# Neighbourhood attention with float16 pairs: probabilities turned by DMA instead of by TensorE

## The chip, the cores and the metric

The kernel runs on one core of one Trainium2 chip. The metric is the device time of one execution, in microseconds (us). The median of three runs before the change is 1503.19 us (1502.85 to 1503.6). The engines are PE (TensorE, matrix products; PEld is its weight load), DVE (VectorE), ACT (ScalarE), POOL (GpSimd) and SP (SyncE, which issues nearly all DMAs here, from one queue in order).

## The reference, cut to what matters

One layer of an encoder trunk on 1024 tokens of width 1024. Its token mixer has two halves, an mLSTM and a neighbourhood attention; their outputs are joined in one output projection. Then come a cross-attention and a gated FFN. Only the neighbourhood attention is changed. The tokens stand on a grid of 16 rows by 64 columns, there are 8 heads of width 64, and each token attends to a window of 8 rows by 16 columns:

```python
qg, kg, vg = grid(nq), grid(nk), grid(nv)
row_idx = jnp.clip(r - kr // 2, 0, rows - kr)[:, None] + jnp.arange(kr)[None, :]
k_rows = kg[:, :, row_idx].reshape(b, NA_HEADS, rows, kr * GRID_W, NA_DIM)
v_rows = vg[:, :, row_idx].reshape(b, NA_HEADS, rows, kr * GRID_W, NA_DIM)
s = jnp.einsum('bhrqd,bhrkd->bhrqk', qg, k_rows) * (NA_DIM ** -0.5)
...
s = jnp.where(mask, s + bias, -jnp.inf)
p = jax.nn.softmax(s, axis=-1)
o = jnp.einsum('bhrqk,bhrkd->bhrqd', p, v_rows)
```

All of it is float32 in the reference.

## The kernel before, in words

The kernel is written with a tile framework: the Python code names tiles and instructions, and a scheduler fixes, when the kernel is built, in which order each engine runs its instructions. At run time every engine goes through its own list in order and waits on semaphores. Products that need more than a 16-bit or a rounded 32-bit operand are made of two parts, high and low (`hi`, `lo`), and three matmuls (`mm3`: high by high, high by low, low by high). `split` makes such a pair with a copy on ACT and a subtraction on DVE; `split16` makes a pair of float16 with a scale `s`: ACT writes `hi = s*src`, DVE writes `lo = s*src - hi`.

The order of the program: layer norm and the token products (`tk`: values `nv`, output gates `mo`), the column products (`cu`, `cl`), the mLSTM, the neighbourhood attention, the second half of the output projection (`out`), the cross-attention, the FFN. Two parts of the program stand beside the change.

**The token products.** For `c` in 0 to 3 and 8 token tiles `tt`, PE makes a 128x256 product `tk`, DVE evicts it to `ev` (L819); for `c` below 2 `ev` is a part of the values and is stored as float32 to `nv` in DRAM.

**The neighbourhood attention** (`na_gen`, L1132 on). It runs over 4 head pairs `p` and 4 column blocks `cb`, 16 jobs in all. A job handles 16 columns of queries of two heads; these need 32 columns of keys. In a job:

- ACT and POOL split the queries (`qsh`, `qsl`) and the 16x32 keys (`kh`, `kl`, once per job) into pairs of float32r, and POOL subtracts bias from mask (`tb`, three jobs in four).
- The values `vt` are fetched with four DMAs (L1177).
- For each of 4 groups `g` of 4 query rows (8, 12, 12 and 8 key rows, so 256 or 384 keys): PE makes the scores `S` with `mm3`; DVE adds the table, takes the minimum of the negated scores and writes `P` (L1189); ACT takes the exponential and its sum (L1191); DVE inverts the sum (L1193) and scales `P` by it (L1194); PE turns `P` around in blocks of 128x128 (`tp`, L1199); ACT copies that to `PT` (L1201); PE multiplies with the values in float32 (`o`, L1203, two instructions each).
- ACT and DVE split the result into the pair `yna` (tiles `X2h`, `X2l`).

`mix` runs the first half of the output projection between these steps as filler for PE (`fill`, 16 products of 12 matmuls; L1072 loads a row tile, L1089 evicts on DVE, L1094 adds a bias on POOL, L1096 stores to `part`). Its second half, `out`, needs all of `yna`: product `k` of a row tile needs head pair `k`. It loads `part` back, and the cross-attention loads 4 MB of `kq` at the same time.

PSUM banks are named by letters: the scores have `Y` (3 banks), `o` has `X` (2), the filler has `Z` (1), and `tp` has 2.

## Time and profile before

| | |
|---|---|
| median of 3 runs | 1503.19 us (1502.85 to 1503.6) |
| profiled execution: its own time | 1502.08 us |
| profiled execution: span | 1500.0 us, so 2.08 us lie around the span |
| PE busy over the span | 1441.3 us (96%) |
| DVE, ACT, POOL busy | 1036.0 (69%), 825.7 (55%), 575.1 us (38%) |
| granted TensorE clock, mean | 0.992 |
| first and last L1189 (softmax) instruction start | 478.7 and 616.5 us |
| L1203 (products with values) | 487.2 to 629.3 us |

How to read it: PE is busy nearly all the time over the whole span, so a mean says little of the changed stage. The views to read are those cut to that stage, about 477 to 631 us, and to the token products, about 123 to 262 us. A row of the groups gives count, busy time and the mean of one instruction; a row of the windows gives the busy time of each engine in a stretch (PE, PEld, DVE, ACT, POOL, each with its count), the granted clock, the DMA share and GB/s; a row of the waits says who waited for whom, for how long in all, how often, and the longest. In the timeline, `xN` joins N like instructions in a row, and the second number is the time from the start of the first to the end of the last; matmuls overlap, so the distance of two starts is the time that one takes of PE.

### The profile page before, as it was taken

How to read it: one execution, taken by the hardware profiler on the slowest of the kernel's cores; microseconds unless marked ns; L12 is line 12 of the kernel's file. 1: busy time of each engine (PE TensorE's matmuls, PEld its weight loads, DVE VectorE, ACT ScalarE, POOL GpSimd, SP SyncE). 2: the span in 40 equal slices, each digit the busy share in tenths (PEclk: the TensorE clock that was granted, in tenths of full speed). 3: DMA queues.
4: the chain of work that ended last, by engine and by line, in shares of the span. 5: the costliest groups of instructions: out<-in, count | busy, mean ns of one | idle time of the engine just before them, and what ended most of it. 6: DMA issues, size and time to landing. Idle time of an engine off the chain costs nothing. (4 is left out here: it accounts for less than half of the span.)

```text
span 1500.0 us, 21659 instructions
## 1 busy us (share of the span) xinstructions
PE 1441.3 (96%) x8060; PEld 867.1 (58%) x8060; DVE 1036.0 (69%) x1945; ACT 825.7 (55%) x1393; POOL 575.1 (38%) x453
## 2 busy tenths in 40 slices
PE   8999999999999898999999799999999999999998
PEld 6998866456766887874444344444444444444444
DVE  7867866545777687488555868887787789707424
ACT  5766565655554666425444777787777767503000
POOL 5452357303325766045112454443444320300543
PEclk9999999999999999999999899999999999999999
DMA  8846653215544633644333233232233336713121
GB/s 308 318 163 215 197 186 129 84 49 151 164 124 156 206 127 127 239 155 71 85 71 100 88 138 126 113 126 113 113 118 119 143 114 239 271 36 99 48 76 59
DMA packets 116383, 208.61 MB, mean 139 GB/s; under 512 B 40627, under 2 KB 69555, under 8 KB 112950
## 3 DMA queue, kind: packets, MB, share of 16 engines
q1 hardware_dynamic: 115984, 206.47, 41.3%
q8 instruction: 63, 1.03, 0.3%
q0 software_dynamic: 144, 0.49, 0.2%
q14 instruction: 42, 0.34, 0.1%
q10 hardware_dynamic: 150, 0.27, 0.0%
HBM read 154.15 MB, written 45.15 MB: 133 GB/s over the span
## 5 line engine op out<-in xcount | busy, mean ns | idle before, releaser
L1527 POOL TENSOR_TENSOR wraw<-ur 128x512 f32<-128x512 f32 x22 | 45.9, 2085 | 207.1 <-issue 192.3
L225 PE MATMUL dn<-wlo,yp 128*128 128x512 f16 (+1 forms) x284 | 105.1, 370 | 0.0
L224 PE MATMUL dn<-whi,yp 128*128 128x512 f16 (+1 forms) x284 | 104.9, 370 | 0.0
L226 PE MATMUL dn<-whi,yp 128*128 128x512 f16 (+1 forms) x284 | 104.4, 370 | 0.0
L1615 DVE SCALAR_TENSOR_TENSOR cbuf<-C,wdw,cbuf 128x1024 f32<-128x1024 f32 x44 | 69.8, 1587 | 35.0 <-ACT cbuf L1614 34.8
L226 PEld LDWEIGHTS <-wlo 128*128 128x128 f16 x540 | 52.8, 98 | 56.5 <-DVE wlo L204 1.3
L225 PEld LDWEIGHTS <-whi 128*128 128x128 f16 x540 | 52.8, 98 | 55.9 <-issue 3.3
L224 PEld LDWEIGHTS <-whi 128*128 128x128 f16 x540 | 52.8, 98 | 53.1 <-ACT whi L203 0.3
L242 POOL TENSOR_TENSOR lnrs<-lnrs,mhalf 128x1 f32<-128x1 f32 x32 | 25.9, 809 | 137.9 <-DVE lnrs L241 132.2
L204 DVE SCALAR_TENSOR_TENSOR wlo<-wraw,us,whi 128x1024 f16<-128x1024 f32 (+1 forms) x48 | 62.5, 1320 | 18.7 <-ACT whi L203 18.7
L1616 DVE SCALAR_TENSOR_TENSOR cbuf<-C,wdw,cbuf 128x1024 f32<-128x1024 f32 x44 | 70.4, 1601 | 0.7
L252 ACT ACTIVATE r<-r,lnrs 128x1024 f32<-128x1024 f32 x19 | 23.6, 1239 | 78.3 <-DVE lnrs L251 78.0
L203 ACT ACTIVATE whi<-wraw,us 128x1024 f16<-128x1024 f32 (+1 forms) x48 | 51.2, 1102 | 16.4 <-DVE us L176 15.5
L225 PEld LDWEIGHTS <-yp 128*128 128x128 f16 x370 | 36.2, 98 | 39.9
L224 PEld LDWEIGHTS <-yp 128*128 128x128 f16 x370 | 36.2, 98 | 39.8
L1614 ACT ACTIVATE cbuf<-C,bdw,wdw 128x1024 f32<-128x1024 f32 x44 | 54.2, 1234 | 9.1 <-DVE C L1652 8.5
L226 PEld LDWEIGHTS <-yp 128*128 128x128 f16 x370 | 36.2, 98 | 39.7
L224 PE MATMUL tk<-whi,Bo 128*128 128x256 f16 (+1 forms) x192 | 52.6, 274 | 2.5 <-DVE stage L204 2.5
L224 PE MATMUL tk<-whi,Be 128*128 128x256 f16 (+1 forms) x192 | 52.6, 274 | 0.7 <-DVE stage L204 0.7
L225 PE MATMUL tk<-wlo,Be 128*128 128x256 f16 (+1 forms) x192 | 52.4, 274 | 0.8 <-DVE wlo L204 0.8
L225 PE MATMUL tk<-wlo,Bo 128*128 128x256 f16 (+1 forms) x192 | 52.5, 274 | 0.0
L226 PE MATMUL tk<-whi,Be 128*128 128x256 f16 (+1 forms) x192 | 52.5, 274 | 0.0
(526 smaller groups left out, 4892.1 us busy)
## 6 DMA issues: line engine op xcount, KB each, us to landing
ur<-in_w_up_dram SPq DMA_DIRECT2D x22, 1024.0 KB
sv<-in_w_down_dram SPq DMA_DIRECT2D x22, 512.0 KB
y<-cbuf SPq DMA_DIRECT2D x22, 512.0 KB
ur<-y SPq DMA_DIRECT2D x11, 1024.0 KB
wraw<-in_w_down_dram SPq DMA_DIRECT2D x22, 512.0 KB
r<-h SPq DMA_DIRECT2D x11, 512.0 KB
wraw<-in_w_tok_dram SPq DMA_DIRECT2D x10, 512.0 KB
wr<-in_w_xk_dram SPq DMA_DIRECT2D x8, 512.0 KB
```

The source lines that it names most:

```text
L203: A.activation(hi, src, AF.Copy, scale=s)
L204: return V.scalar_tensor_tensor(lo, src, s, hi, op0=OP.mult, op1=OP.subtract)
L224: T.matmul(ps, lh, rh, start=first, stop=False, skip_group_check=skip)
L225: T.matmul(ps, lh, rl, start=False, stop=False, skip_group_check=skip)
L226: return T.matmul(ps, ll, rh, start=False, stop=last, skip_group_check=skip)
L242: G.tensor_tensor(rs[:, 0:1], rs[:, 0:1], mhalf[:, 0:1], OP.pow)
L252: A.activation(r, r, AF.Identity, scale=rs[:, 0:1], bias=rs[:, 1:2])
L1527: G.tensor_tensor(S1, A21, A22, OP.add)
L1614: A.activation(c, C[:, 1:SEQ + 1], AF.Identity, scale=wdw[:, 1, j:j + 1], bias=bdw[:, j:j + 1])
L1615: V.scalar_tensor_tensor(c, C[:, 0:SEQ], wdw[:, 0, j:j + 1], c, op0=OP.mult, op1=OP.add)
L1616: V.scalar_tensor_tensor(c, C[:, 2:SEQ + 2], wdw[:, 2, j:j + 1], c, op0=OP.mult, op1=OP.add)
```

## The change

It makes these edits.

- Probabilities and values become float16 pairs. The scaling of `P` by the inverse sum (L1194) and the turning on PE (L1199) and the copy to `PT` (L1201) go. In their place `split16` writes `hl`, high and low, with the inverse sum times 2^14 as its scale, once for every two groups; and two DMA transposes per job, issued from SP, turn `hl` (128x1280 float16 each) to `PT`.
- The products with values go by key block: four blocks of 128 keys per job, each with all the groups that use it (256 or 384 columns), three float16 matmuls each. They run for job n-2 while job n is in work (`pv_gen`, yielded after the scores of job n).
- The values are brought to float16 pairs in the token stage: their largest magnitude is taken from `ev` (16 reductions on DVE), then each token tile is read back, split and written to a new scratch `nvp` (`nv_pair`, 8 times), laid out so that one DMA of 128 rows of 2 KB serves a job (`pv_load`, 16 in place of 64).
- The keys are split once per head pair (128x1024) and not once per job (128x512). The low part overwrites the raw tile.
- The filler has the two `tp` banks beside `Z`; it loads and stores its rows later (`late`); the second half of the output projection begins three row tiles with the products that need head pairs 0 to 2 (`lead`).

The diff, cut to its core:

```diff
-               fill="Z", fill2="ZX", ...
+               fill=["Z", "tp", "tp"], ...
+                    def nv_pair(tt):
+                        ...
+                        S.dma_start(f, nv_d[rows, :])
+                        hl = w1.tile([128, 4, 2, 128], F16, name="nvhl", tag="nvhl", bufs=2)
+                        split16(hl[:, :, 0], hl[:, :, 1], f.rearrange("p (k d) -> p k d", k=4), nvs[0][1])
+                        S.dma_start(... nvp_d ..., hl.rearrange("p k n d -> p k (n d)"))
                             if c < 2:
                                 S.dma_start(nv_d[tt * 128:(tt + 1) * 128, j], e)
+                                V.tensor_reduce(nvm[:, 8 * c + tt:8 * c + tt + 1], e, axis=mybir.AxisListType.X,
+                                                op=OP.max, apply_absolute_value=True)
+                            if c == 2 and tt == 1:
+                                nvs.append(scale_of(nvm, 14))
+                            if 8 * c + tt in range(18, 26):
+                                nv_pair(8 * c + tt - 18)
...
+            def pv_gen(n):
+                ...
+                for b in range(4):
+                    s0, g0, g1 = BG[b]
+                    vh, vl = vt[:, b, 0], vt[:, b, 1]
+                    ph, pl = (PT[:, i, s0:s0 + g1 - g0] for i in range(2))
+                    T.matmul(po[:, g0:g1], vh, ph, start=b == 0, stop=False, skip_group_check=True)
+                    T.matmul(po[:, g0:g1], vh, pl, start=False, stop=False, skip_group_check=True)
+                    anchor[0] = T.matmul(po[:, g0:g1], vl, ph, start=False, stop=b == 3, skip_group_check=True)
+                    yield 1
...
-                        kh = nw.tile([128, 16, 32], F32R, name="kh", tag="kh", bufs=2)
-                        kl = nw.tile([128, 16, 32], F32R, name="kl", tag="kl", bufs=2)
-                        A.activation(kh, kr[:, :, k0:k0 + 32], AF.Copy)
-                        (V if n < 2 else G).tensor_tensor(kl, kr[:, :, k0:k0 + 32], kh.bitcast(F32), OP.subtract)
+                        if cb == 0:
+                            kh = nw.tile([128, 16, 64], F32R, name="kh", tag="kh", bufs=2)
+                            kl = kr.bitcast(F32R)
+                            A.activation(kh, kr, AF.Copy)
+                            (V if n < 1 else G).tensor_tensor(kl, kr, kh.bitcast(F32), OP.subtract)
...
-                            V.reciprocal(mn[:, 1:2], mn[:, 1:2])
-                            V.tensor_scalar(P[:, :nk], P[:, :nk], mn[:, 1:2], None, op0=OP.mult)
+                            Ps.append((P, nk, m, g))
+                            if g % 2:
+                                V.reciprocal(mn[:, 1], mn[:, 1])
+                                V.tensor_scalar(mn[:, 1], mn[:, 1], 2.0 ** 14, None, op0=OP.mult)
+                                for P, nk, m, g_ in Ps:
+                                    nb = nk // 128
+                                    o = slice(GSLOT[g_], GSLOT[g_] + 2 * nb - 1, 2)
+                                    split16(hl[:, 0, o], hl[:, 1, o], P[:, :nk].rearrange("p (b t) -> p b t", b=nb),
+                                            m[:, 1])
-                            for b in range(nb):
-                                T.transpose(pt[:, b, :], P[:, b * 128:(b + 1) * 128], ident)
-                            A.activation(PT[:, :nb, :], pt[:, :nb, :], AF.Copy)
-                            for b in range(nb):
-                                anchor[0] = T.matmul(po[:, g, :], vt[:, r0 // 4 + b, :], PT[:, b, :], start=b == 0,
-                                                     stop=b == nb - 1)
+                        pts[n] = PT = nw.tile([128, 2, 10, 128], F16, name="PT", tag="PT", bufs=2)
+                        for i in range(2):
+                            S.dma_start_transpose(PT[:, i], hl[:, i].rearrange("p b t -> p (b t)"))
+                        if n > 1:
+                            yield from pv_gen(n - 2)
...
-            run(out_half(wB, ylk(yna), part0_d, None, None, "out", after1, todo=todo, home=home))
+            run(out_half(wB, ylk(yna), part0_d, None, None, "out", after1, todo=todo, home=home, lead=3))
```

The instruction lists of the two kernels differ most in three places. The first is DVE in the middle of the attention. Before, after each exponential DVE inverts one sum (L1193) and scales one `P` (L1194); the rows named ISA are the L1189 step and the reading of its minimum:

```order
L1189 ISA mn 128x1
L1193 RECIPROCAL mn<-mn 128x1
L1189 ISA P,mn<-S,tb_0_5428 128x256
L1189 ISA mn 128x1
L1194 TENSOR_SCALAR P<-P,mn 128x384
L1193 RECIPROCAL mn<-mn 128x1
L1194 TENSOR_SCALAR P<-P,mn 128x256
L1193 RECIPROCAL mn<-mn 128x1
L1194 TENSOR_SCALAR P<-P,mn 128x256
L1189 ISA P,mn<-S,tb_1_5429 128x384
```

Now the same place on DVE (L205 is the second instruction of `split16`, L1126 the eviction of the filler):

```order
L1277 RECIPROCAL mn<-mn 128x2
L1278 TENSOR_SCALAR mn<-mn 128x2
L205 SCALAR_TENSOR_TENSOR hl<-P,mn,hl 128x3x128
L205 SCALAR_TENSOR_TENSOR hl<-P,mn,hl 128x2x128
L1271 ISA P,mn<-S,tb_1_5511 128x384
L1271 ISA mn 128x1
L205 SCALAR_TENSOR_TENSOR X2l<-o,sc,X2h 64x16x16
L1271 ISA P,mn<-S,tb_3_5512 128x256
L1271 ISA mn 128x1
L1126 SCALAR_TENSOR_TENSOR r<-r,fill 128x512
L205 SCALAR_TENSOR_TENSOR hl<-P,mn,hl 128x2x128
L205 SCALAR_TENSOR_TENSOR hl<-P,mn,hl 128x3x128
```

One scaling of `P` per group has become one low part per group, which reads `P` and the high part and mostly stands next to that of the pair's other group, and one inversion with one small scaling now serve two groups.

The second place is SP's queue in the second half of the attention. Before:

```order
L1177 DMA vt<-nv 128x1x128 x4
L1096 DMA part_73<-r 128x1024
L1177 DMA vt<-nv 128x1x128 x3
L1072 DMA r<-h_72 128x1024
L1177 DMA vt<-nv 128x1x128 x7
L1096 DMA part_73<-r 128x1024
```

Now, at a like place:

```order
L1288 DMA_TRANSPOSE PT<-hl 128x10x128 x2
L1130 DMA part_73<-r 128x1024
L1213 DMA vt<-nvp 128x1x1024
L1094 DMA r<-h_72 128x1024
L1288 DMA_TRANSPOSE PT<-hl 128x10x128 x2
L1213 DMA vt<-nvp 128x1x1024
L1288 DMA_TRANSPOSE PT<-hl 128x10x128 x2
```

Four loads of values per job have become one, and two transposes per job, which wait for ACT's and DVE's parts of `hl`, stand between the loads and stores of the filler.

The third place is SP's queue at the end of the attention. Before, the 4 MB of `kq` stand behind the last loads of values:

```order
L1380 DMA whi<-vo 128x2048
L1380 DMA wlo<-vo 128x2048
L1177 DMA vt<-nv 128x1x128 x4
L1253 DMA kq_7242<-kq 128x4096 x2
L1253 DMA kq_7243<-kq 128x4096 x2
```

Now they stand behind the last four transposes:

```order
L1463 DMA wlo<-vo 128x2048
L1288 DMA_TRANSPOSE PT<-hl 128x10x128 x2
L1213 DMA vt<-nvp 128x1x1024
L1288 DMA_TRANSPOSE PT<-hl 128x10x128 x4
L1336 DMA kq_6991<-kq 128x4096 x2
L1336 DMA kq_6992<-kq 128x4096 x2
```

On PE, 27 matmuls of `out` and the products of jobs 13 and 14 now stand between the last scores and the products of job 15, and 36 of the 192 matmuls of `out` stand ahead of those; 18 more follow them that need only head pairs 0 to 2.

More of the change, by code (lines that the diff above doesn't have):

```diff
@@ L1058, in out_w, with out_half @@
                     for k in range(4)]
-        def out_half(w, y, res, dst, work, name, after=None, bias=None, rbufs=3, early=False, alpha=ALPHA, todo=range(NT), home=None):
+        def out_half(w, y, res, dst, work, name, after=None, bias=None, rbufs=3, early=False, alpha=ALPHA, todo=range(NT), home=None, late=False, lead=0):
             rs = {}
@@ L1074, in out_half, with part @@
             load_r(todo[0])
+            if late:
+                load_r(todo[1])
             yield 0
+            done, begun = [], {}
+            def part(ps, tt, ch, ks):
+                for k in ks:
+                    yh, yl = y(k, tt)
+                    wh, wl = w[k]
+                    cc = slice(ch * 512, ch * 512 + 512)
+                    mm3(ps, yh, yl, wh[:, 0, cc], wl[:, 0, cc], k == 0, k == 3)
+            for tt in todo[:lead]:
+                for ch in range(2):
+                    begun[tt, ch] = bank(name)
+                    part(begun[tt, ch], tt, ch, range(3))
             for n, tt in enumerate(todo):
-                if n + 1 < NT:
+                if n + 1 < NT and not late:
                     load_r(todo[n + 1])
@@ L1080, in out_half @@
                 for ch in range(2):
-                    ps = bank(name)
-                    for k in range(4):
-                        yh, yl = y(k, tt)
-                        wh, wl = w[k]
-                        cc = slice(ch * 512, ch * 512 + 512)
-                        mm3(ps, yh, yl, wh[:, 0, cc], wl[:, 0, cc], k == 0, k == 3)
+                    if (tt, ch) in begun:
+                        ps = begun[tt, ch]
+                        part(ps, tt, ch, (3,))
+                    else:
+                        ps = bank(name)
+                        part(ps, tt, ch, range(4))
                     rc = r[:, ch * 512:ch * 512 + 512]
@@ L1091, in out_half @@
                         V.tensor_tensor(rc, ps, rc, OP.add)
+                    if done and ch == 0:
+                        S.dma_start(*done.pop())
+                    if late and ch == 1 and 0 < n < NT - 1:
+                        load_r(todo[n + 1])
                     yield 1
@@ L1095, in out_half @@
                 if dst is not None:
-                    S.dma_start(dst[tt * 128:(tt + 1) * 128, :], r)
+                    done.append((dst[tt * 128:(tt + 1) * 128, :], r))
+                    if not late or n == NT - 1:
+                        S.dma_start(*done.pop())
                 if after is not None:
@@ L1220, in out_a @@
                 yield from out_half(wA, ylk(yml), h0_d, part0_d, nw,
-                                    "fill", bias=bmo, rbufs=2, early=True)
+                                    "fill", bias=bmo, rbufs=2, early=True, late=True)
                 with tc.issue_after(vload[0].ins):
```

83 lines of the change are left out of this document (55 added, 28 removed).

## The prediction, blind

> **What bounds the kernel now.** I cut the profile to the stages that the change touches and read the windows first. Columns: stretch, its length, then busy time and count of PE, PEld, DVE, ACT and POOL, granted clock, DMA share, GB/s.
>
> ```profile
> 123.00:195.00 72.00, 68.18 (x609) 59.31 (x608) 59.10 (x129) 40.61 (x67) 24.56 (x34) 1.00 0.61 192
> 195.00:262.00 67.00, 64.34 (x466) 45.55 (x465) 43.47 (x76) 36.51 (x71) 46.67 (x59) 1.00 0.45 158
> 478.70:618.50 139.80, 126.11 (x807) 113.57 (x806) 107.92 (x310) 91.07 (x259) 87.56 (x84) 0.98 0.45 148
> 618.50:631.00 12.50, 11.17 (x74) 9.85 (x73) 1.88 (x6) 3.54 (x9) 0.00 (x0) 1.00 0.85 334
> ```
>
> The third row is what I call the front: from the first softmax step to the last scaling of `P`. PE is busy 126.1 of 139.8 us (90%), DVE 107.9 (77%), ACT 91.1 (65%), POOL 87.6 (63%). So PE has the most work, but it does not fill the front. The fourth row is the tail: DVE is done, and PE still turns and multiplies. Next the chief waits from 477 to 632 us:
>
> ```profile
> ACT P L1191 <- DVE mn L1189: 25.8, 16, 5.4
> ACT PT L1201 <- PE tp L1199: 19.4, 16, 3.4
> DVE mn L1193 <- ACT P L1191: 12.4, 26, 1.3
> PEld S L224 <- DVE mn L1189: 10.9, 9, 4.7
> PE S L224 <- DVE mn L1189: 8.8, 6, 4.5
> ```
>
> DVE and ACT wait for each other, ACT waits for PE's transposes, and where PE stops it is for DVE, which has not yet emptied a bank of scores. So PE and DVE both hold the front. Less work for PE pays only as far as DVE can follow.
>
> **PE: -26.4 us, mostly off the path afterwards.** Starts in the timeline give what one instruction takes of PE (the second number includes the drain):
>
> ```profile
> 616.08 0.40 PE L226 MATMUL out<-whi,X2l 128*128 128x512 f32 x1
> 616.31 0.40 PE L224 MATMUL out<-whi,X2h 128*128 128x512 f32 x1
> ...
> 624.05 0.49 PE L1199 MATMUL tp<-ident,P 128*128 128x128 f32 x3
> 624.38 0.61 PE L1203 MATMUL o<-PT,vt 128*128 128x128 f32 x4
> 624.82 0.49 PE L1199 MATMUL tp<-ident,P 128*128 128x128 f32 x3
> ...
> 665.96 0.39 PE L224 MATMUL S<-kq,h1T 128*128 128x512 f16 x1
> 666.18 0.38 PE L225 MATMUL S<-kq,h1T 128*128 128x512 f16 x1
> ```
>
> A matmul of `out` takes 0.23 us. Three transposes take 0.33 us and four records of the float32 product 0.44, so 0.11 each. A job has 10 and 20 of them: 3.3 us go. The new products of a job have (256+384+384+256) x 3 = 3840 columns, and a float16 matmul of 512 columns takes 0.22 us: 1.65 us come. That is -1.65 us a job and -26.4 in 16 jobs. PE's share of the front falls from 126 to about 100 us, so I expect another engine to set it.
>
> **DVE: the scaling goes, a dearer low part comes.** The rows of both forms (first the groups of the front, then the tile `P` over the whole program, with min/median/max, then one undisturbed instruction):
>
> ```profile
> L1194 DVE TENSOR_SCALAR P<-P,mn 128x256 f32<-128x256 f32 x32 | 24.2, 757 | 1.0
> L1194 DVE TENSOR_SCALAR P<-P,mn 128x384 f32<-128x384 f32 x32 | 22.6, 707 | 0.7
> L1189 DVE CUSTOM_DVE_ANT_0 P<-S,tb 128x384 f32<-128x384 f32 x32 | 17.4, 551 | 1.3 <-PE tp L1199 1.1
> L1189 DVE CUSTOM_DVE_ANT_0 P<-S,tb 128x256 f32<-128x256 f32 x32 | 13.2, 416 | 3.6 <-PE S L226 2.6 <-PE tp L1199 0.9
> L1193 DVE RECIPROCAL mn<-mn 128x1 f32<-128x1 f32 x64 | 10.1, 159 | 12.7 <-ACT P L1191 12.4
> ...
> L1194 DVE TENSOR_SCALAR P<-P,mn x64: 353/566/2337, 480.2 to 618.4; 128x256 f32<-128x256 f32 x32, 128x384 f32<-128x384 f32 x32
> L203 ACT ACTIVATE Ps<-P,mn x32: 491/496/508, 679.9 to 809.8; 128x256 f16<-128x256 f32 x32
> L204 DVE SCALAR_TENSOR_TENSOR Ps<-P,mn,Ps x32: 470/483/2194, 683.9 to 810.4; 128x256 f16<-128x256 f32 x32
> 546.98 0.42 DVE L1194 TENSOR_SCALAR P<-P,mn 128x384 f32<-128x384 f32 x1
> ```
>
> The scalings cost 24.2 + 22.6 = 46.8 us, though undisturbed they would take 32 x 0.353 + 32 x 0.42 = 24.7; 22.1 us, or 0.345 each, are something else. The cross-attention has the new form already, the low part `Ps`: 0.48 us for 256 columns. For 384 I add what the softmax step adds for 128 columns (0.551 - 0.416 = 0.135): 0.62. So 64 low parts take 32 x 0.48 + 32 x 0.62 = 35.2 us undisturbed. In place of 64 inversions of 0.16 come 32 inversions and 32 scalings of a 128x2 tile, as small: 0. The something else is POOL:
>
> ```profile
> 683.94 0.47 DVE L204 SCALAR_TENSOR_TENSOR Ps<-P,mn,Ps 128x256 f16<-128x256 f32 x1
> 684.10 2.52 POOL L1306 TENSOR_TENSOR r<-r,vec 128x1024 f32<-128x1024 f32 x1 [1.16 <-DVE r L1305]
> 684.94 1.96 DVE L204 SCALAR_TENSOR_TENSOR Ps<-P,mn,Ps 128x256 f16<-128x256 f32 x1
> ```
>
> The same low part takes 0.47 us where it begins before POOL's addition, and 1.96 where it begins inside it: it comes out shortly after POOL's end at 686.62. The softmax step and the inversion show no such spread. So the low parts wait for POOL as the scalings did, and the 32 small scalings, the same operation as L1194, may too: 96 chances instead of 64. At the old 0.345 each that is 33 us. I take 24, for two reasons. POOL loses key splits:
>
> ```profile
> L1174 POOL TENSOR_TENSOR kl<-kr,kh 128x512 fp32r<-128x512 f32 x12 | 15.8, 1316 | 0.5
> ```
>
> 15 of 1.3 us become 3 of twice the width, 19.7 us become 7.9, 14% of POOL's 87.6: 33 becomes 28.6. [...] With half of the 64 free of it, 64 x 0.345 x 0.86 = 19. Between 19 and 28.6 stands 24. DVE in the front: 107.9 - 46.8 + 35.2 + 24 = 120.3 us, 12 more than before.
>
> [...]
>
> **ACT: +2.7 us, off the path.** It loses the copies to `PT` and three quarters of the key copies:
>
> ```profile
> L1201 ACT ACTIVATE PT<-tp 128x384 f32<-128x384 f32 x32 | 15.3, 480 | 6.7 <-PE tp L1199 6.5
> L1201 ACT ACTIVATE PT<-tp 128x256 f32<-128x256 f32 x32 | 11.8, 374 | 13.0 <-PE tp L1199 12.9
> L1173 ACT ACTIVATE kh<-kr 128x512 fp32r<-128x512 f32 x12 | 7.6, 632 | 0.7 <-PE S L226 0.4
> ```
>
> It gains 64 high parts: 32 x 0.496 (the row `Ps` above) and 32 x 0.60 (with the copies' 0.106 for 128 columns), 35.1 us against 27.1; the key copies go from 16 x 0.63 to 4 x 1.2, -5.3. From 91.1 to 93.8 us: it stays behind DVE. What it no longer does is wait 19.4 us for PE's transposes with exponentials queued behind.
>
> **The front.** DVE now has 120.3 us of work, PE 100, ACT 94, POOL about 76. Before, the busiest engine reached 90% of the front. I take the same for DVE: 120.3 / 0.9 = 133.7 us, against 139.8: **-6.1**.
>
> **The start: +1.** The first key split, twice as wide, runs on ACT and DVE ahead of the first scores (0.63 and about 1.2 us more); PE has filler to do meanwhile, but DVE's first step moves by about 1 us.
>
> **The transposes and SP's queue: 0, with a cover.** A transpose of 128x1024 holds SP for half of its row here, and lands about 2 us later:
>
> ```profile
> 693.08 3.22 SPq L1417 DMA_TRANSPOSE PTe<-Ps  x2
> ...
> L226 PEld LDWEIGHTS <-PTe x32: 96/98/98, 698.3 to 728.6; 128*128 128x128 f16 x32
> ```
>
> The second, out of SP by 696.30, is used at 698.3. With 128x1280 that makes about 1.55 to 2 us each of SP, at most 64 us in all; 48 loads of values fall away. SP stays under half of the front, and the product runs two jobs behind, some 16 us, against 5 us for two transposes. Queued behind a transpose that waits for DVE are the filler's loads and stores and the next values; they too are a job early. If that cover goes, PE waits for `PT`.
>
> **The tail: -3.** Before:
>
> ```profile
> 616.93 2.31 SPq L1253 DMA_DIRECT2D kq<-kq  x4
> ...
> 629.59 3.93 SPq L1072 DMA_DIRECT2D r<-part  x8
> ...
> 638.58 0.50 PE L224 MATMUL out<-whi,X2h 128*128 128x512 f32 x1 [1.06 <-DVE r L1091]
> ```
>
> From 618.5 us to the first scores of the cross-attention, at 665.96, are 47.5 us. Now, from the last low part: transpose and landing 3.6 us, in which PE has its 27 matmuls of `out` at 0.23 and two jobs of products (9 us from the last scores); product of job 15 1.65; then 192 - 36 = 156 matmuls of `out`, 35.9 us. Sum 41.1. But the 4 MB of `kq` go out only behind the last transpose, and the rows of `part` behind them: 12.5 us at the 334 GB/s of the tail's row, 1.5 for the first row, so DVE can empty a bank of `out` some 16 us after the last low part, and PE needs one at 13.5: +2.5. That is 43.6, 4 less than 47.5; I take 3, since the last jobs' waits can only grow. Bounds: +3 (all six banks wait for late rows) to -6 (the rows are in time).
>
> **The token products: +2.5.**
>
> ```profile
> L594 DVE TENSOR_REDUCE sums<-xk 128x1 f32<-128x256 f32 x8 | 3.2, 406 | 0.6 <-ACT xk L593 0.6
> ...
> L204 DVE SCALAR_TENSOR_TENSOR wlo<-ev,us,whi x6: 740/748/1757, 265.9 to 301.0; 128x512 f16<-128x512 f32 x6
> ```
>
> DVE gets 16 reductions of 0.41, 6.5 us, in the window from 123 to 195, where it is busy 59 of 72 us and PE loses 3.8; and 8 low parts of 0.75, 6 us, with as many high parts on ACT, 8 loads and 8 stores on SP's queue, from 195 to 262, where DVE is busy 43 of 67. Most lies beside PE. Bounds: 0, and 12.5 if all is seen. From DVE's 82% in the first window I take 1.5, and 1 for the second, where the new stores wait in SP's queue ahead of weight loads.
>
> **The sum:** -6.1 + 1 - 3 + 2.5 = -5.6. On the profiled execution's 1502.08 us that gives 1496.5; the median of the runs stands 1.1 us higher, so I predict 1497.6, and call it 1498. A difference under 0.2% (3 us) can hardly be told from none.
>
> **Rivals.** (a) DVE follows much better, since ACT is free of PE: POOL's wait falls to 16 us and DVE fills 95%: (96.3 + 16) / 0.95 = 118, -21.6 in the front, -21 in all: 1482. If the whole 26.4 us of PE came through it would be 1477. For it: the 19.4 us wait that goes. Against it: the small scalings' new exposure. (b) Slower, by one mechanism: POOL's hold on DVE. At the old rate of 0.345 us on all 96 chances DVE has 96.3 + 33 = 129.3 us, the front takes 143.7, +3.9; its late end costs the tail's gain, the start and the tokens stay: +7.4, or 1511. It decides from 0.30 us per chance: there (96.3 + 29) / 0.9 = 139.2 and the gain is gone. [...] (c) The change works but SP's queue holds: a transpose waiting for DVE blocks rows and values, PE waits once a few jobs and the last product is late; 6 us eat the gain: 1503.
>
> **Chances and range.** The forecast 0.40, (a) 0.20, (b) 0.25, (c) 0.15. Faster by over 0.2%: 0.32 of the forecast, 0.20 of (a), 0.02 of (c), 0.54. Slower: 0.03 of the forecast, 0.22 of (b), 0.05 of (c), 0.30. The rest, 0.16, within. The likeliest case alone spans 1490 to 1505 (tail and tokens at their bounds); with (a) and (b) the range is 1481 to 1512.
>
> **What would show it.** In the profile after: L1194, `tp` in the front and `PT` copies gone, PE near 100 us in the front with waits on DVE; DVE near 90%, the low parts `hl` at a mean of 0.75 to 0.9 us with maxima over 2; the small scalings well over 0.16. PE waiting for `PT` would speak for (c); `hl` at 0.55 for (a). The sum fails if the front does not follow DVE at all, for instance if the clock or the order of PE sets it.

## The result, and the profile after

The changed kernel takes 1530.84 us (median of 4 runs, 1528.44 to 1532.34), the kernel before on the same chip 1503.39 us: a ratio of 1.0179, 95% interval 1.0162 to 1.0197. It is slower by 27.5 us, where 5.6 us of gain were forecast and 1512 us was the upper end of the range. The profiled spans differ by a little more, 1529.7 against 1500.0 us.

The marks of the stages (first and last starts of their instructions) say where the 29.7 us of the spans arose:

| stage | before | after | change | forecast |
|---|---|---|---|---|
| to the last column product (`cl`), by the token products | 470.1 us | 479.6 us | +9.5 | +2.5 |
| from there to the first softmax step (start) | 8.6 | 12.4 | +3.8 | +1 |
| first softmax step to last scaling or low part (front) | 139.7 | 158.3 | +18.6 | -6.1 |
| from there to the first scores of the cross-attention (tail) | 47.6 | 48.7 | +1.1 | -3 |
| all behind | 834.0 | 830.7 | -3.3 | 0 |

No stage came out as forecast. The windows of after, cut like those of before (stretch, length, busy time and count of PE, PEld, DVE, ACT, POOL, granted clock, DMA share, GB/s):

```profile
123.00:195.00 72.00, 65.71 (x575) 56.94 (x574) 62.40 (x136) 38.39 (x64) 22.31 (x30) 0.95 0.59 185
195.00:262.00 67.00, 63.54 (x461) 45.56 (x459) 43.17 (x83) 37.96 (x72) 45.62 (x57) 0.95 0.63 206
492.00:650.90 158.90, 113.39 (x534) 86.17 (x533) 107.29 (x309) 98.95 (x253) 74.73 (x68) 0.85 0.92 184
650.90:663.40 12.50, 10.43 (x56) 7.74 (x55) 2.55 (x6) 1.88 (x4) 0.00 (x0) 1.00 1.01 316
```

Read the third row against the front of before. DVE has as much work as it had (107.3 against 107.9 us) but 19 us more in which to do it: it fills 68% of the front, where it filled 77% before and the prediction had 90%. PE is busy 113.4 us. ACT is at 62%. No engine is the bound, so the front is made of waits. Two columns have moved far: the DMA share from 0.45 to 0.92, and the granted clock from 0.98 to 0.85. The chief waits from 470 to 690 us (who waited for whom: us in all, times, longest):

```profile
DVE mn L1277 <- ACT P L1273: 25.6, 16, 7.8
...
PE o L1195 <- DMA PT<-hl: 23.4, 10, 5.3
ACT P L1273 <- DVE mn L1271: 17.9, 12, 7.5
...
PE S L225 <- DVE mn L1271: 15.2, 4, 8.2
...
ACT kh L1254 <- DMA kr<-nqk: 12.9, 2, 9.4
...
DVE hl L205 <- ACT hl L204: 9.7, 7, 4.3
```

Rows between engines tell of a ring in which each waits for the next. The rows that start the ring end in "DMA": PE waits for `PT`, ACT waits for `kr`. Both can be followed in the timeline. First job 2 (the two transposes stand as one row on SP):

```profile
528.66 1.01 DVE L205 SCALAR_TENSOR_TENSOR hl<-P,mn,hl 128x384 f16<-128x384 f32 x2
...
529.05 7.58 SPq L1288 DMA_TRANSPOSE PT<-hl  x2
...
537.71 0.37 PE L1195 MATMUL o<-PT,vt 128*128 128x256 f16 x1 [5.28 <-DMA PT<-hl]
```

The last low parts of the job end at 528.66 + 1.01 = 529.67 us, and PE wanted the product at 537.71 - 5.28 = 532.43. So the cover was 2.8 us. "Two jobs behind" counts PE's scores, which run ahead of DVE: by 529.67 us PE had issued 17 groups of scores, five past the twelve of jobs 0 to 2. And the two transposes took 8.0 us from the last low part to the product, of which SP was held for 7.58 from the first one's start. Over the 16 jobs the cover, from the last low part to the moment when PE was ready for the product, is 2.2 to 10.5 us, 4.5 in the median. Then the key copy of pair 1, which stands on ACT before the exponentials of job 1:

```profile
489.70 1.32 SPq L1234 DMA_DIRECT2D kr<-nqk  x1
...
491.81 1.03 SPq L1234 DMA_DIRECT2D kr<-nqk  x1
...
506.29 1.06 ACT L1254 ACTIVATE kh<-kr 128x1024 fp32r<-128x1024 f32 x1 [9.37 <-DMA kr<-nqk]
```

The first of these rows is pair 1, the second pair 2. The keys of pair 1 come some 16 us after their row on SP begins, among the loads of the start; until then nothing behind them on ACT runs, though the keys are not needed for three more jobs. The first transpose is issued at 512.2 us, so this wait is not of its making.

### The profile page after: what moved, and what is told of

The parts are those of the page before. It is cut to its first block, busy times and chain, and to the rows that moved or that the text cites. A ratio compares the mean times of both kernels' runs of the same rounds, so it can differ in the third digit from the quotient of the medians.

```text
span 1529.7 us, 21213 instructions
## 1 busy us (share of the span) xinstructions
PE 1435.3 (94%) x7774; PEld 841.6 (55%) x7774; DVE 1046.9 (68%) x1975; ACT 836.1 (55%) x1389; POOL 567.2 (37%) x441
## 3 DMA queue, kind: packets, MB, share of 16 engines
q1 hardware_dynamic: 157008, 221.15, 47.3%
## 5 line engine op out<-in xcount | busy, mean ns | idle before, releaser
L1698 DVE SCALAR_TENSOR_TENSOR cbuf<-C,wdw,cbuf 128x1024 f32<-128x1024 f32 x44 | 70.3, 1597 | 35.2 <-ACT cbuf L1697 35.1
L205 DVE SCALAR_TENSOR_TENSOR wlo<-wraw,us,whi 128x1024 f16<-128x1024 f32 (+1 forms) x48 | 62.7, 1324 | 17.5 <-ACT whi L204 17.5
L243 POOL TENSOR_TENSOR lnrs<-lnrs,mhalf 128x1 f32<-128x1 f32 x32 | 24.9, 778 | 134.2 <-DVE lnrs L242 128.4
L253 ACT ACTIVATE r<-r,lnrs 128x1024 f32<-128x1024 f32 x19 | 23.6, 1240 | 87.2 <-DVE lnrs L252 87.0
L204 ACT ACTIVATE whi<-wraw,us 128x1024 f16<-128x1024 f32 (+1 forms) x48 | 51.1, 1102 | 14.9 <-DVE us L177 14.7
L225 PE MATMUL tk<-whi,Bo 128*128 128x256 f16 (+1 forms) x192 | 53.3, 278 | 0.7 <-DVE stage L205 0.7
L227 PE MATMUL tk<-whi,Bo 128*128 128x256 f16 (+1 forms) x192 | 53.2, 277 | 0.0
L225 PE MATMUL tk<-whi,Be 128*128 128x256 f16 (+1 forms) x192 | 52.6, 274 | 0.0
```

The costliest lines, as they stand in the source:

```text
L204: A.activation(hi, src, AF.Copy, scale=s)
L205: return V.scalar_tensor_tensor(lo, src, s, hi, op0=OP.mult, op1=OP.subtract)
L225: T.matmul(ps, lh, rh, start=first, stop=False, skip_group_check=skip)
L227: return T.matmul(ps, ll, rh, start=False, stop=last, skip_group_check=skip)
L243: G.tensor_tensor(rs[:, 0:1], rs[:, 0:1], mhalf[:, 0:1], OP.pow)
L253: A.activation(r, r, AF.Identity, scale=rs[:, 0:1], bias=rs[:, 1:2])
```

## The experiments

My theory after these readings was: (T1) the transposes make the front slow. The ways in which they could do so are rivals of each other: their DMA time (small packets), their place in SP's queue, or their lateness for an order of PE that leaves no cover. (T2) POOL's hold on DVE, rival (b) of the prediction, sets the front. (T3) The token additions cost on their own what the trace says. All kernels were timed against the kernel before; where a ratio stands in brackets it is the 95% interval.

**The token additions alone.** The kernel before, with the reductions, the scale and the pairs (the diff shown above under "The change", its part in the token products); `nvp` is not read.

> The kernel before plus only the token-stage additions: the 16 reductions, the scale, and the eight pairs of values with their stores to nvp, which nothing reads. The prediction's term was +2.5 us, so about 1505.7. The trace of the changed kernel has the first column product 9.5 us later, so by my theory now (two idle stretches of PE of about 4 us, each followed by a lower granted clock) about 1512 to 1513. If the time stays within 3 us of 1503, the 9.5 us of the trace were lost to something else.

Measured: 1510.24 us, ratio 1.0051 [1.0036, 1.0066], +7.8 us. Then the same with the pairs left out:

```diff
-                            if 8 * c + tt in range(18, 26):
-                                nv_pair(8 * c + tt - 18)
```

> The kernel before plus the 16 reductions of the values and their scale alone, without the pairs. All token additions cost 7.8 us. The prediction had 1.5 of 2.5 us for the reductions. If DVE's 16 steps of 0.4 us cause the first idle stretch of PE (4.3 us and the lower clock behind it), 1506 to 1509; if the pairs are most of it, 1503 to 1505.

Measured: 1505.07 us, 1.0014 [1.0003, 1.0025], +2.5 us. T3 holds: 7.8 of the 27.5 us have nothing to do with the attention. It is the second case of the expectation, at its upper edge: the reductions are some 2.5, the pairs the other 5. The idle stretch of PE is there with the reductions alone, so it is worth no more than their 2.5 us (waits of PE, 140 to 175 us, in that kernel):

```profile
PE mem L225 <- DVE stage L205: 4.3, 1, 4.3
```

The changed kernel's timeline shows what such a stretch does:

```profile
160.19 0.27 PE L227 MATMUL tk<-whi,Be 128*128 128x256 f16 x1
164.75 0.37 PE L225 MATMUL mem<-xkp,whi 128*128 128x256 f16 x1 [4.29 <-DVE stage L205]
164.92 0.42 PE L226 MATMUL mem<-xkp,whi 128*128 128x256 f16 x1
165.13 0.42 PE L227 MATMUL mem<-xkp,wlo 128*128 128x256 f16 x1
```

PE stands 4.3 us because DVE is late with `stage`. After it, matmuls start 0.21 us apart and not 0.11, until 169.6, 4.9 us in all; the granted clock from 164.7 to 169.7 us was 0.50. After the waits of 1.6 and 1.7 us at this place before the change, the spacing stayed at 0.11. The pairs do the like at a second place: ACT stands at a pair whose load is late, with weight splits behind it, PE runs short, and the clock falls (waits of 215 to 245, then two windows):

```profile
ACT nvhl L204 <- DMA nvf<-nv: 5.2, 1, 5.2
```

```profile
220.00:230.00 10.00, 6.54 (x48) 4.52 (x46) 9.50 (x13) 6.04 (x11) 5.54 (x6) 0.89 0.89 264
230.00:240.00 10.00, 10.00 (x56) 5.88 (x55) 6.97 (x13) 6.47 (x12) 7.05 (x9) 0.77 0.89 303
```

At the second place no single wait is as long as the 4.3 us at the first: three of 0.8, 0.8 and 1.9 us stand within 5.2 us, and behind them, from 229.4 to 234.4 us, matmuls of 512 columns start 0.43 us apart and not 0.21, at a granted clock of 0.50.

**No transposes.** `PT` is two tiles filled once.

```diff
-                        pts[n] = PT = nw.tile([128, 2, 10, 128], F16, name="PT", tag="PT", bufs=2)
-                        for i in range(2):
-                            S.dma_start_transpose(PT[:, i], hl[:, i].rearrange("p b t -> p (b t)"))
+                        pts[n] = PTc[n % 2]
```

> The changed kernel without its 32 transposes in the neighbourhood attention: PT are two tiles filled once with a constant, so this part of the output is not computed from the probabilities; all else runs. If the transposes (their traffic, their lateness, their place in SP's queue) cost the front its 19 us and more, the front falls from 158.7 us to 134 to 140 and the time to 1506 to 1512. If POOL's hold on DVE is what slows the front, it stays above 150 us and the time above 1522.

Measured: 1514.93 us, 1.0079 [1.0064, 1.0094]; 15.9 us come back, a little less than expected. But this kernel leaves out more than the transposes. With `PT` filled ahead, the products wait for nothing in the front, and the scheduler put the first of them ahead of the first softmax step (first and last starts):

```profile
L1198 PE MATMUL o<-PT,vt x64: 269/326/527, 492.7 to 583.7; 128*128 128x256 f16 x32, 128*128 128x384 f16 x32
...
L1274 DVE CUSTOM_DVE_ANT_0 P<-S,tb x64: 401/476/558, 502.3 to 637.0; 128x256 f32<-128x256 f32 x32, 128x384 f32<-128x384 f32 x32
```

In the changed kernel the products start from 515.8 to 656.8 us. So the start takes 23.2 us here (12.4 in the changed kernel), the front 138.1 and the tail 41.5; start and front together take 161.3 us, against 170.7 in the changed kernel and 148.3 before. T1 holds as far as this goes: most of the loss hangs on the transposes, or on the products' wait for them, which went with them. T2 does not hold for the changed kernel: POOL's hold is here nevertheless, and larger. The groups and the window of this front:

```profile
L205 DVE SCALAR_TENSOR_TENSOR hl<-P,mn,hl 128x384 f16<-128x384 f32 x32 | 25.4, 797 | 2.0 <-ACT hl L204 1.6
L205 DVE SCALAR_TENSOR_TENSOR hl<-P,mn,hl 128x256 f16<-128x256 f32 x32 | 25.2, 791 | 1.0 <-ACT hl L204 0.8
...
L1281 DVE TENSOR_SCALAR mn<-mn 128x2 f32<-128x2 f32 x32 | 14.9, 465 | 0.9
```

```profile
502.30:641.00 138.70, 114.62 (x548) 87.22 (x547) 118.96 (x310) 99.65 (x253) 72.68 (x65) 0.89 0.38 127
```

Here DVE is what the prediction said it would be: 119.0 us of work (forecast 120.3), of which 25.4 + 25.2 + 14.9 - 35.2 - 32 x 0.16 = 25.2 us are the hold (forecast 24). But start and front together are 13 us longer than before the change, so the 26 us that PE works less by the prediction's estimate do not show even where nothing waits for `PT`. A part of the 13 us is the early products' own doing (PE waits 5.3 us for `vt` ahead of the first softmax step), so this is no clean measure of what the front could reach.

**Which property of the transposes?** Plain copies in their place, and, apart from it, the other loads and stores of the front moved from SP's to ACT's queue (`S.dma_start` to `A.dma_start` for `vt`, `wide`, `qr`, `kr` and the filler's rows):

```diff
-                            S.dma_start_transpose(PT[:, i], hl[:, i].rearrange("p b t -> p (b t)"))
+                            S.dma_start(PT[:, i].rearrange("p b t -> p (b t)"), hl[:, i].rearrange("p b t -> p (b t)"))
```

> The changed kernel with each transpose in the neighbourhood attention replaced by a plain DMA copy of the same tile from hl to PT, from the same place in SP's queue and with the same waits; PT then holds the probabilities unturned, so this part of the output is another. If what costs is the transposing itself (packets under 512 bytes, DMA time, late landing), the time comes within 4 us of the kernel without transposes, 1506 to 1515. If what costs is that SP's queue waits for hl in order with other loads and stores behind it, it stays at 1524 or above.

> The changed kernel with the other DMAs of the front (values, filler's rows in and out, queries, keys, bias rows) issued from ACT's queue, so that SP's queue there holds the transposes and little else. If SP's order is the cost, 10 us or more come back, 1520 or less. If the transposes' own DMA time is the cost, the time stays within 4 us of 1530.8, or rises by what ACT pays for issuing some 44 DMAs.

Measured: copies 1531.81 us, 1.0193 [1.0178, 1.0209], no gain at all; loads on ACT's queue 1539.09 us, 1.0253 [1.0233, 1.0272], 8 us worse. The first was a surprise, for the copies do relieve the DMA engines. Two windows of the changed kernel, and the same two with copies:

```profile
520.00:560.00 40.00, 31.52 (x150) 23.88 (x149) 27.62 (x79) 27.30 (x70) 19.85 (x20) 0.81 0.97 162
560.00:600.00 40.00, 27.59 (x141) 20.63 (x140) 27.43 (x80) 23.96 (x63) 24.21 (x24) 0.95 1.03 180
```

```profile
520.00:560.00 40.00, 29.88 (x145) 22.99 (x143) 31.62 (x77) 26.32 (x68) 22.07 (x21) 0.87 0.54 173
560.00:600.00 40.00, 28.54 (x134) 20.72 (x135) 28.26 (x81) 24.59 (x64) 18.21 (x20) 0.87 0.55 164
```

The DMA share falls from 1.0 to 0.55, PE and DVE get no more done by their counts, and PE still waits for `PT`:

```profile
PE o L1195 <- DMA PT<-hl: 20.4, 8, 4.1
```

So in this order of the work DMA time is not what the front lacks (the tail is 3.7 us shorter with copies, the front 3.6 us longer). The expectation's other reading, SP's queue, has the second run against it: with the queue nearly their own, the transposes still kept PE waiting 22 us for `PT` and ACT 13.7 us for a free `hl`, and ACT now stood at loads as well (9.9 us for `kr`). That kernel also gives ACT the issuing, so it does not clear SP's order of all blame. The reading that is left is lateness: transposes and copies alike land after PE wants them. The next runs try it.

**Give the product a cover, and take `kh` out of the way.** Two holds, alone and together. The first holds a job's first product on PE until the scores of the third job after it are issued (with three `PT` buffers); the second holds `kh` on ACT:

```diff
-                        if n > 1:
-                            yield from pv_gen(n - 2)
+                        if n > 2:
+                            yield from pv_gen(n - 3, anchor[0])
```

```diff
-                            A.activation(kh, kr, AF.Copy)
+                            with (tc.issue_after(exps[4 * n - 5].ins) if n else nullcontext()):
+                                A.activation(kh, kr, AF.Copy)
```

> The changed kernel with the products of a job held on PE until all scores of the third job after it are issued (three PT buffers in place of two; queries of pair 2 in the vector tile, to make room). In the changed kernel a product stands 2.8 jobs of scores behind its own, some 7 us behind the end of its low parts, and PE waits 28 us for PT in the front. If this lateness sets the front, PE's waits for PT fall under 5 us and the time to 1518 to 1524. If DMA time or SP's order sets it, PE's wait turns into another (ACT for a free hl) and the time stays within 4 us of 1530.8.

> The changed kernel, but the key copy kh of head pairs 1 to 3 is held on ACT until the exponentials of the job two before its own are issued. In the changed kernel kh of pair 1 stands on ACT behind job 0 and waits 9.4 us for kr, with four exponentials behind it. If that wait is a cost of its own, 5 to 9 us come back: 1522 to 1526. If the time is set by PE's wait for PT further on, it stays within 4 us of 1530.8.

> Both of the last two edits in one kernel. If the two waits (ACT for kr at the start, PE for PT after) are what the front lost, this comes to the kernel without transposes, 1512 to 1518, though all transposes run. If the transposes cost by their traffic or their queue, 1522 or more.

Measured: 1526.08, 1523.71 and 1530.84 us (1.0154 [1.0138, 1.0169], 1.0143 [1.0124, 1.0162], 1.0189 [1.0172, 1.0206]). `kh` late gave the 7 us expected; that is a cost of the key split in this order of the work and not of the transposes. The third job gave 4.8 us, less than expected, although its wait was gone, from 28.3 us (rows of `PT` in that kernel):

```profile
  DMA PT<-hl: 3.1, 2
```

Both together gave nothing, against the expectation. The trace shows a new stop at 603 us, and that it is of the same kind:

```profile
603.36 0.17 DVE L1282 RECIPROCAL mn<-mn 128x2 f32<-128x2 f32 x1 [0.54 <-ACT P L1278]
609.24 1.22 DVE L197 TENSOR_REDUCE sc<-vec 128x1 f32<-128x1024 f32 x1 [5.71 <-DMA vec<-in_ln_w_dram]
```

A reduction of the next stage's norm weights stands in DVE's list between softmax steps, and its load is queued on SP behind transposes. DVE waits 5.7 us for a number that only the next stage wants, and PE stood 10.4 us behind DVE.

**Take such steps away too.** First the norm's bounds, then also the scaling of a bias row and two weights' low parts (POOL makes them instead):

```diff
-            p1, s1 = pow2(ln_bound(lw, lb)[1], 14)
+            with tc.issue_after(lo_last[0].ins):
+                p1, s1 = pow2(ln_bound(lw, lb)[1], 14)
...
-                    wB.extend(out_w("w_mix_out", 4, (V, None, V, None)))
+                    wB.extend(out_w("w_mix_out", 4))
...
-        V.tensor_scalar(bxo, bxo, 1.0 / ALPHA, None, op0=OP.mult)
+        with tc.issue_after(lo_last[0].ins):
+            V.tensor_scalar(bxo, bxo, 1.0 / ALPHA, None, op0=OP.mult)
```

> The kernel with both holds (products three jobs behind, kh late), and the bounds of the layer norm's weights (reductions of vec and wb on DVE) held behind the last low part. With both holds alone DVE stood 5.7 us at the reduction of vec, whose load is queued on SP behind transposes, and PE 10.4 us behind DVE. If the front loses its time to whichever engine's list has an early step that waits for a late DMA, this comes to 1514 to 1522. If there is a cost of the transposes beside such waits, the time stays at 1526 to 1534.

> The kernel with all holds (products three jobs behind, kh late, the norm's bounds behind the last low part), and two more steps taken out of DVE's list in the front: the scaling of the bias row vec, held behind the last low part, and the low parts of two weights, given to POOL. In the kernel with three holds DVE still stood 3.9 and 5.3 us at these. If such steps are what is left, the time falls from 1523 to 1516 to 1520. If the transposes' DMA time is what is left, it stays at 1521 to 1525.

> The same with plain copies of the same tiles in place of the transposes, so PT holds the probabilities unturned and this part of the output is another. In the changed kernel that swap halved the DMA share of the front and left the time. With the waits held away, DMA time could show: if the small packets of the transposes are a cost, 4 us or more below the kernel with transposes; if not, within 2.5 us of it.

Measured: 1523.22 us (1.0133 [1.0112, 1.0155]), 1520.91 us (1.0116 [1.0097, 1.0135]) and, with copies, 1512.61 us (1.0059 [1.0042, 1.0077]). The first two are 7.6 and 9.9 us below the changed kernel, where `kh` late alone had given 7.1. The first falls between its two cases; the second is 0.9 us above its lower case and at the edge of the other, and the two intervals overlap. So stops of this kind were a part, not all. And now that the order no longer hides it, the DMA time shows: copies are worth 8.3 us, where they had been worth none. It lies not in the front, which is 145.9 us in both, but in the tail: 51.5 us with transposes, 43.6 with copies. Windows of the tail, with transposes and then with copies:

```profile
640.00:650.00 10.00, 8.88 (x43) 6.84 (x43) 3.35 (x13) 1.70 (x4) 0.00 (x0) 1.00 1.00 363
650.00:660.00 10.00, 4.27 (x14) 3.02 (x13) 3.44 (x11) 0.00 (x0) 0.00 (x0) 0.81 1.02 405
```

```profile
640.00:650.00 10.00, 8.69 (x43) 6.54 (x42) 4.44 (x15) 1.79 (x4) 0.00 (x0) 1.00 0.99 405
650.00:660.00 10.00, 9.02 (x41) 7.07 (x40) 7.77 (x24) 0.70 (x1) 0.57 (x1) 1.00 1.03 402
```

There the DMA engines are full in both (share 0.99 to 1.03): 4 MB of `kq`, the rows of `part` and the last transposes want them at once, and with transposes PE is busy 4.3 us out of 10. A small load behind them (`wb`) is late too: SP issues it at 642.2 us and DVE has it at 655.6, with copies at 641.0 and 651.6. A product in PE's list waits for what DVE makes of it:

```profile
PE mx L183 <- DVE sc L189: 4.7, 1, 4.7
```

From 650 us on the granted clock is 0.81 and then 0.85 in two stretches of 10 us, with copies 1.00 in both. With copies PE's list has no such wait in the tail. So the DMA time costs here by way of one more early step; how much of the 8.3 us stays when that step is held too was not tried.

The front with all holds is 8 us longer than the 138.1 without transposes, but that kernel's start is 11 us longer: start and front together are 158.2 us here and 161.3 there. That is still 10 us more than before the change. In this front PE waits almost only for DVE (29.6 of its 35.6 idle us), and DVE's low parts and small scalings carry 33.2 + 22.5 + 11.7 - 40.3 = 27.1 us of POOL's hold, with copies 34.0 + 24.9 + 12.3 - 40.3 = 30.9 (40.3 is what they would take undisturbed; a low part takes 0.87 us in the mean, with copies 0.92). So with the DMA waits gone the hold of T2 is back. No kernel without the hold was made; what it costs there stays open.

**The keys alone.** The kernel before with one part of the change, keys split once per head pair; then with `kh` held as above; then with the `lead` of the output projection too (`out_half` and its last call as in the change, `lead=3`).

```diff
-                        A.activation(kh, kr[:, :, k0:k0 + 32], AF.Copy)
-                        (V if n < 2 else G).tensor_tensor(kl, kr[:, :, k0:k0 + 32], kh.bitcast(F32), OP.subtract)
+                        if cb == 0:
+                            kh = nw.tile([128, 16, 64], F32R, name="kh", tag="kh", bufs=2)
+                            kl = kr.bitcast(F32R)
+                            A.activation(kh, kr, AF.Copy)
+                            (V if n < 2 else G).tensor_tensor(kl, kr, kh.bitcast(F32), OP.subtract)
```

> The kernel before with one part of the change alone: keys split once per head pair, the low part over the raw tile. The prediction's terms for it were +1 us at the start against 5 us less of ACT and 12 us less of POOL off the path: 1502 to 1505. If ACT's wait for kr of pair 1, which stands just as early on ACT here, costs as in the changed kernel, 1507 to 1512.

> The kernel before with keys split once per head pair, and kh of pairs 1 to 3 held on ACT until the exponentials of the job two before. Keys alone gave 1497.7 with ACT waiting 8.4 us for kr in two places. If that wait costs here as in the changed kernel (7 us), 1490 to 1494; if PE has its own work beside it here, 1496 to 1499.

> The same with the lead of the output projection added: six products begin with head pairs 0 to 2 ahead of the last job. The prediction took 3 us for the tail of the changed kernel. If the tail waits for the last head pair, 3 us less than the kernel with keys held; if it waits for the rows of part and the banks, the same within 2 us.

Measured: 1497.73 us (0.9963 [0.995, 0.9976]), 1495.92 us (0.9958 [0.9944, 0.9972]) and 1495.85 us (0.9955 [0.9939, 0.9972]). The key split is a gain of 5.6 us by itself, better than expected; of the 4.0 us between the profiled spans 1.6 lie in the front and 2.5 behind the tail. Its wait for `kr` is in the trace here too:

```profile
ACT kh L1174 <- DMA kr<-nqk: 8.4, 2, 7.3
```

Taking that wait away is worth at most 2 us here, within the intervals, where it was worth 7 in the changed kernel. That PE has its turning and products to do in between is the expectation's reading, and fits, but was not tried apart. The lead is worth nothing here: the tail stays at 47.6 us, so six products begun earlier do not shorten it. The kernel with keys and held `kh` beats both kernels: the one before by 0.42% (0.28% to 0.56%), the changed one by 2.3% of the medians.

## Why the prediction was wrong, step by step

- **The transposes "0, with a cover".** This step failed, and it is the largest part of the loss: without the transposes, and the wait for them, 15.9 of the 27.5 us come back. The cover was taken from the program's words, two jobs, 16 us; it was 2.2 to 10.5 us, 4.5 in the median. The order had to be read from the low part: when DVE ended job 2's low parts, PE had issued 17 groups of scores, five past the job's own last. The need was undersized too. Two transposes were put at 5 us and took 8.0 in job 2. One holds SP for 1.3 to 5.3 us, 82 us in all 32, where the prediction had at most 64 (its 1.55 us for one is a slip; half of its row is 1.61). The mechanism was that of rival (c), at 6 us there. More cover alone, the third job, gave 4.8 us.
- **ACT "off the path".** This failed too. The key copies were priced by their time on ACT, -5.3 us, and the wait of the first of them for its keys at nothing. It was 9.4 us with exponentials behind it, and holding `kh` alone gave 7.1 us.
- **Where the prices stand.** From the medians: token additions 7.8; order, with all holds, 1530.84 - 1520.91 = 9.9; DMA time of the transposes 1520.91 - 1512.61 = 8.3; together 26.0 of the 27.5 us. That the three add up is an assumption: they were measured on different kernels, the third was worth nothing until the second was gone, and inside the second `kh` late gave 7.1 alone, the third job 4.8 alone, and both together nothing.
- **The front, -6.1.** DVE's work and POOL's hold came out as forecast in the kernel without transposes; the 90% did not. DVE fills 68% of the front of the changed kernel, and 86% where nothing waits for `PT`, and even there start and front together are 13 us longer than before. The change took PE's work out of a front that PE did not hold alone, and the granted clock of the front was 0.85 where it had been 0.98: PE is busy 113.4 us and not 100. At full clock that would be 113.4 x 0.85 = 96 us by estimate, so its work was about what the prediction said and the clock made the rest. Rival (a) needed DVE at 95%; no run came above 86%.
- **POOL's hold, 24 us, and rival (b).** The low parts take 0.79 us in the mean in the kernel without transposes, against 0.48 and 0.62 undisturbed. That they wait for POOL shows in the changed kernel: the 18 that begin inside an instruction of POOL take 0.61 to 2.58 us, 1.06 in the mean, and each ends 0.28 to 0.54 us after that instruction; the other 46 take 0.47 to 0.62. The small scalings take 0.17 to 1.84 us inside and 0.15 to 0.17 otherwise, so their exposure was rightly counted. But the 24 us lean on the 19 in which half of the low parts were free of POOL, and no run shows that the second of two is spared: of the 19 low parts that follow another at once in the changed kernel four begin inside an instruction of POOL and take 0.89 to 2.58 us, of the 45 others 14 begin so. The groups of low parts and small scalings come there to 23.6 + 20.3 + 9.6 us, 13.2 of them hold, and it did not set the time. With all holds and copies it is 30.9 us, or 0.32 for each of the 96 chances, which is beyond the 0.30 from which rival (b) had the gain gone. So rival (b) is not refuted.
- **The token products, +2.5.** The terms of DVE were right (0.41 and 0.75 us), but the step took "beside PE" for granted at 82% of DVE, and left out the clock, which went from 1.00 to 0.95 in both windows: the additions cost 7.8 us alone. Its upper bound, 12.5, held.
- **The start, +1.** The trace has +3.8, and not from the key split: with keys alone the start is 8.6 us as before. Ahead of the first softmax step stand two more evictions of the filler (489.39 and 491.37 us), which has three banks now. That reading was not tried apart.
- **The tail, -3.** The 43.6 us of the prediction are, by coincidence, what the kernel with held order and copies has, which has no transposes. With transposes the tail is 47.1 to 51.5. The row with a DMA share of 0.85 was shown in the prediction: the term that was missing is the DMA time that the transposes of the last jobs add to a stage that was nearly full, and the small load that comes late behind it. That `lead` helps was wrong by itself, as the kernel with keys shows.
- **Behind the tail** the changed kernel is 3.3 us shorter. The kernel with keys alone is 2.5 us shorter there as well, and those with the token additions alone are not, so it goes with the key split and not with the transposes; what does it stays open.

## What to carry to other kernels

When a step is moved from an engine to a DMA, count the time between the last write of its source and the place of its first reader in that reader's own list, not the jobs between them in the program; if the reader's engine runs ahead of the writer's, the cover is smaller than the jobs say, here 2.2 to 10.5 us in place of 16. Look then at what stands early in every in-order list and waits for a load in the same queue, because each such step can stop a ring of engines, and mending one can uncover the next. A kernel that leaves out a DMA leaves out a dependence too: look where the scheduler then puts the reader before a stage's length is compared. Work taken from the busiest engine need not gain where that engine does not hold the stage alone; here the one part that took work from engines without adding a DMA, the key split, was the gain.

## What the runs showed of the hardware

The 32 transposes here (128x1280 float16, SBUF to SBUF) cost the DMA engines 3.0 to 3.5 times as much time as copies of the same bytes. Page lines on packets and on SP's queue, with all holds, first with transposes and then with copies:

```profile
DMA packets 157406, 223.27 MB, mean 147 GB/s; under 512 B 82675, under 2 KB 107507, under 8 KB 153974
...
q1 hardware_dynamic: 157008, 221.15, 47.7%
```

```profile
DMA packets 120030, 223.26 MB, mean 148 GB/s; under 512 B 41203, under 2 KB 66035, under 8 KB 116598
...
q1 hardware_dynamic: 119632, 221.15, 43.9%
```

The queue moves the same 221.15 MB. Its packets took 47.7% of 1519.1 us with transposes, 724.6 us of all 16 engines, and 43.9% of 1512.2 us with copies, 663.9. Without either (42.3% of 1512.1 us, 210.66 MB) it was 639.6, in a kernel that has none of the holds. By these differences 32 copies of 0.33 MB took 24 us, 0.76 each, and 32 transposes 85 us, 2.7 each, with 37,376 packets more in all and 41,472 more under 512 bytes. In the order of the changed kernel the queue's packets took 47.3% of 1529.7 us, 723.6, and with copies 43.7% of 1528.6, 668.0: 28 us for the copies and 84 for the transposes, 3.0 times as much. On SP a transpose took 1.3 to 5.3 us (1.9 in the median) in the changed kernel, a copy in its place 0.5.

The granted clock was lower where PE had more waits, taken over the front: 0.98 with PE busy 90% of the time before, 0.85 with 71% in the changed kernel. So part of the work that PE was spared it paid back at the lower clock. In shorter stretches it did not go by the busy share alone: 0.81 with PE at 79% from 520 to 560 us, 0.95 at 69% from 560 to 600.
